# Queueing the weight-block sums of a decoder layer behind the attention's loads and products

## The chip, the cores and the metric

The kernel runs on one core of a Trainium2 chip. The metric is the device time of one launch in microseconds (us), lower is better. Times are medians of several runs. Profiles come from single executions, so each has its own time beside that median.

TensorE (PE) multiplies matrices and loads their weights (PEld), VectorE (DVE) and GpSimd (POOL) work elementwise, ScalarE (ACT) evaluates functions, and SyncE (SP) issues most of the DMA transfers. Each engine takes its instructions in the order of its own queue.

## The reference

One decoder layer in float32, with 2048 tokens of 1024 channels:

```python
a = rmsnorm(h, g_pre_mix);  u = a @ w_in
conv_out = swish(layernorm(causal_depthwise_conv(val * sigmoid(gate), width 31)))
attn_out = rmsnorm(stick_breaking(q, k, v))            # 8 heads of 64
h = h + rmsnorm(concat(conv_out, attn_out) @ w_out, g_post_mix)
f = rmsnorm(h, g_pre_ffn)
h = h + rmsnorm((silu(f @ w_gate) * (f @ w_up)) @ w_down, g_post_ffn)
```

Stick-breaking attention has no softmax. The weight of key s for query t is sigmoid(z_ts) times the product of 1 − sigmoid(z_tj) over the keys j between s and t. The feed-forward part has 2816 inner channels, so w_gate and w_up are 1024 × 2816 and w_down is 2816 × 1024.

## The kernel before

**Precision.** Float32 products are made from three matmuls: each operand is split into a rounded high part H and the rest L (ACT makes H, POOL or DVE makes L), and H·H + H·L + L·H is summed in PSUM.

**The feed-forward part** multiplies 2 × 2 blocks by a scheme of seven block products instead of eight. That takes sums and differences of blocks of the weights. For w_gate and w_up they are made early, by `sums` (line 839), while the attention runs. For each of 11 pairs j of column tiles and each of the two weights there is a group: `piece` (line 841) loads blocks of 128 × 512, 256 KB, into tiles with the tag `sum`, of which there are three (line 843 issues the load on SP's queue), `combine` (line 848) adds or subtracts two of them in place on POOL (line 849), and `flush` stores the result in DRAM (through `part`, line 777, on SP). A group is four loads, four combinations and four stores, so there are 88 of each. The blocks of the feed-forward part read the results back (line 1044).

**The attention.** `attn(g)` (line 536 and on) works through four groups g of 512 queries, eight heads each, and for each head through the key groups c from g down to 0. A pair of head and key group is called a unit; there are 8, 16, 24 and 32 units in the four groups, 80 in all. `fetch` (line 550) loads K and V of a unit on SP (lines 553 and 554), each with two buffers. `scores` (line 557) multiplies on PE (565, 566), takes two sigmoids on ACT (571, 573), a running product on DVE (575), and multiplies both on POOL (576), with small copies on POOL around it (570, 578). `values` (line 583) transposes the result on PE (592), splits it (249 on ACT, 250 on DVE) and multiplies it with V (597, 598).

**The convolution.** `taps` runs 31 multiply-adds per channel group on DVE (line 478), and `convnorm` (line 485) normalizes four token tiles, one after another: PE transposes (491), ACT and DVE, POOL (192, 193, 503), PE transposes back (508). All four go through one PSUM bank. The output projection of the convolution's half (691 to 693) needs the result of its group.

**What sets the order.** The program is traced in an order written by hand. PLAN lists the main stages with costs; the running sum of those costs is the position, from 0 to about 930. Three side streams, attention, taps and sums, are advanced beside the main stages, so that each has reached a given share of its own work at a given position: ATTN from 0 at position 46 to 1 at 850, SUMS from 0 at 330 to 1 at 900. Steps of the attention are traced before steps of the sums at each point.

From the traced order a scheduler lays out each engine's queue, using a simulated timeline. An instruction that can run and whose buffer is free may be put ahead of instructions that were traced before it. `tc.keep_in_program_order` holds some instructions to the traced order. The sums read only inputs, so in the queues nothing but their tiles holds them back.

The functions that the diff touches:

Of the kernel before, what the change touches and what calls it, by code (L numbers as in the profile page):

```python
# [9 lines left out]
F32 = mybir.dt.float32  # L10
# [3 lines left out]
ALU = mybir.AluOpType  # L14
# [14 lines left out]
G = 512  # L29
# [109 lines left out]
def layer_kernel(ctx: ExitStack, tc: tile.TileContext, x, xT, g_pre_mix, w_in, conv_w, conv_b, ln_g, ln_b,  # L139
                 attn_g, w_out, g_post_mix, g_pre_ffn, w_gate, w_up, w_down, g_post_ffn, out):  # L140
    nc = tc.nc
# [161 lines left out]
    for c in range(CB):  # L303
        t = vp.tile([P, PAD + G], F32, name=f"glu{c}")
# [5 lines left out]
    vd = {}  # L310
# [225 lines left out]
    def attn(g):  # L536
# [13 lines left out]
        def fetch(h, c):  # L550
            K = ap.tile([P, G], F32R, tag="K", name="K")
            V = ap.tile([P, G], F32R, tag="V", name="V")
            nc.sync.dma_start(K.bitcast(F32), kd[h, c].bitcast(F32))
            nc.sync.dma_start(V.bitcast(F32), vd[h // 2, c][:, h % 2, :].bitcast(F32))
            return dict(h=h, c=c, K=K, V=V, A=[])

        def scores(u, j):
            hd_ = heads[u["h"]]
            diag = u["c"] == g
            w = (j + 1) * P if diag else G  # L560
            K = u["K"]
            z = pp.tile([P, G], F32, tag="z", name="z")
            late = g == NG - 1 and u["h"] >= NH // 2
            js = slice(j * P, (j + 1) * P)
            nc.tensor.matmul(z[:, 0:w], hd_["QL"][:, js], K[:, 0:w], start=True, stop=False)
            nc.tensor.matmul(z[:, 0:w], hd_["QH"][:, js], K[:, 0:w], start=False, stop=True)
            if diag:
                nc.vector.tensor_tensor(z[:, w - P:w], z[:, w - P:w], msk, ALU.add)  # L568
            om = ap.tile([P, G + 9], F32, tag="om", name="om", bufs=NOM)
            nc.gpsimd.tensor_copy(om[:, G:G + 1], hd_["prev"][j])  # L570
            nc.scalar.activation(om[:, G - w:G], z[:, 0:w], AF.Sigmoid, scale=-0.125)  # L571
            a = ap.tile([P, G], F32, tag="A", name="A", bufs=NA)
            nc.scalar.activation(a[:, 0:w], z[:, 0:w], AF.Sigmoid, scale=0.125)  # L573
            r = om[:, G - w:G + 1][:, ::-1]
            nc.vector.tensor_tensor_scan(r, r, (one if late else z[:, 0:1]).to_broadcast([P, w + 1]), one, ALU.mult, ALU.bypass)  # L575
            nc.gpsimd.tensor_tensor(a[:, 0:w], a[:, 0:w], om[:, G - w + 1:G + 1], ALU.mult)  # L576
            pv = sp.tile([P, 1], F32, tag="pv", name="pv", bufs=8)
            nc.gpsimd.tensor_copy(pv, om[:, G - w:G - w + 1])
            hd_["prev"][j] = pv
            u["A"].append(a)  # L580
            return w
# [56 lines left out]
        for n in range(len(units) + 1):  # L638
            u = None
            if n < len(units):  # L640
                h, c = units[n]
                if c == g:
                    yield need(("q", g, h // 2), ("k", g, h // 2), ("v", g, h // 2))
                    heads[h] = begin(h)
                u = fetch(h, c)
            for i in range(TT):
                w = 0
                if u is not None:
                    w += scores(u, i)
                if last is not None:  # L650
                    w += values(last, i)
                later = [(k - 1, fn, a) for k, fn, a in later]
                while later and later[0][0] <= 0:
                    _, fn, a = later.pop(0)
                    if fn is back and g > 1:
                        yield need(("mix", g - 2))
                    fn(a)
                yield w
            if last is not None and last["c"] == 0:
                h = last["h"]  # L660
                oT = ap.tile([P, G], F32, tag="oT", name="oT", bufs=1)
                nc.scalar.activation(oT, heads[h]["o"], AF.Copy)
                heads[h]["oT"] = oT
                later.append((FOLD, fold_halves, h))
                if h % 2:
                    later.append((BACK, back, h))
            last = u
# [3 lines left out]
            fn(a)  # L671
        done.add(("attn", g))

    ys = {}

    def outproj(g, part):
# [92 lines left out]
    def store(t, *key, eng=nc.sync):  # L769
        stored[key] = dp.tile([P, *t.shape[1:]], F32, name="_".join(str(k) for k in key))  # L770
        eng.dma_start(stored[key], t)

    def part(t, k, n, *key, eng=nc.sync):

        if key not in stored:
            stored[key] = dp.tile([P, n, G], F32, name="_".join(str(k) for k in key))
        eng.dma_start(stored[key][:, k, :], t)
# [61 lines left out]
    def sums():  # L839

        def piece(w, j, e):
            t = fup.tile([P, G], F32, tag="sum", name="sum", bufs=3)
            nc.sync.dma_start(t, w[j][:, e * G:(e + 1) * G])
            return t

        late = []

        def combine(c, a, b, op, *key):
            nc.gpsimd.tensor_tensor(c, a, b, op)  # L849
            late.append((c, *key))  # L850

        def flush(n):
            while len(late) > n:
                t, kind, *key, m = late.pop(0)
                if kind == "S":
                    ns = (6, 7) if m in (6, 7) else (5, 3)
                    part(t, ns.index(m), 2, kind, *key, ns)
                else:
                    store(t, kind, *key, m)

        for j in range(HF):
            for i, w in enumerate(W):
                a21, a22, a11 = piece(w, j + HF, 0), piece(w, j + HF, 1), piece(w, j, 0)
                yield 1
                combine(a22, a21, a22, add, "S", i, j, 5)
                yield 1
                combine(a21, a21, a11, sub, "S", i, j, 7)
                combine(a11, a22, a11, sub, "S", i, j, 6)
                yield 1
                flush(0)  # L870
                a12 = piece(w, j, 1)
                yield 1
                combine(a12, a12, a11, sub, "S", i, j, 3)
                yield 1
                flush(0)
# [111 lines left out]
    with ExitStack() as E:  # L987
# [10 lines left out]
        e = [(ep, f"e{i}") for i in range(6)]  # L998
# [450 lines left out]
```

## Time and profile before

| | before |
|---|---|
| median of 3 runs | 2525.97 us (2524.9 to 2527.77) |
| the profiled execution, its own time | 2525.87 us |
| its span, first to last instruction | 2523.9 us |
| mean granted clock of PE | 0.981 |
| PE busy | 2392.2 us, 95% of the span |
| DVE, POOL, ACT busy | 1796.9, 1522.1, 1291.7 us |
| DMA | 657.31 MB, mean 260 GB/s |

The attention's units run from 64 to 1470 us of the span, beside the input projection (15 to 889), the output projection of each group and the first block products of the feed-forward part (c11, 915 to 1101 and 1284 to 1464, and p4, 1166 to 1256). After that come the remaining block products of w_gate and w_up (from 1517 to 2084) and those of w_down (2084 to 2514).

In a row of instructions, `L849` is the line of the kernel, `sum<-sum` the tile written and the tiles read, and `x88` the count. Idle time before a group is the time in which the engine had nothing running ahead of its instructions, with what ended it behind the arrow. PEclk, the granted clock, is the share of full speed at which TensorE was clocked in that stretch.

### The profile page before, as it was taken

To read this page: it belongs to the slowest core of one execution; us is meant where nothing else is said; L and a number is where in the kernel's file an instruction comes from. 1 tells how busy PE (TensorE), PEld (TensorE's weight loads), DVE (VectorE), ACT (ScalarE), POOL (GpSimd) and SP (SyncE) were. 2 spreads that over 40 slices of the span, in tenths; PEclk is the share of its full clock that TensorE was granted. 3 is DMA by queue.
4 is the path that set the end of the run, shared out by engine and by line. 5 is a ranking of instruction groups with operands and counts; after the bars stand their busy time and mean duration, and the time that the engine had idled before them with its cause. 6 is when DMAs were issued, how large, how long until landed. Compare 5 with 4: busy or idle time off the path is not lost. (4 is left out here: it accounts for less than half of the span.)

```text
span 2523.9 us, 35648 instructions
## 1 busy us (share of the span) xinstructions
PE 2392.2 (95%) x11156; PEld 1951.2 (77%) x11156; DVE 1796.9 (71%) x2321; ACT 1291.7 (51%) x2398; POOL 1522.1 (60%) x1845
## 2 busy tenths in 40 slices
PE   7989989998899999999989998999999999999998
PEld 6878777775687877888778877777788887887886
DVE  5797579886899887777877536776666654557556
ACT  4554565655565575676666745333332234445443
POOL 5764678547563376637745408765666674558656
PEclk9999999998899999999999999999999999999999
DMA  9989887987576689765677686987878767668765
GB/s 353 319 292 319 287 265 267 353 282 239 185 275 207 205 304 348 240 228 199 235 270 226 212 284 226 345 281 245 311 278 284 273 239 269 192 195 263 251 188 179
DMA packets 289181, 657.31 MB, mean 260 GB/s; under 512 B 33888, under 2 KB 42080, under 8 KB 288992
## 3 DMA queue, kind: packets, MB, share of 16 engines
q1 hardware_dynamic: 264704, 622.01, 73.2%
q10 hardware_dynamic: 24288, 33.04, 3.6%
q8 instruction: 88, 1.44, 0.2%
q14 instruction: 101, 0.83, 0.1%
HBM read 460.92 MB, written 193.99 MB: 259 GB/s over the span
## 5 line engine op out<-in xcount | busy, mean ns | idle before, releaser
L576 POOL TENSOR_TENSOR A<-A,om 128x512 f32<-128x512 f32 (+2 forms) x320 | 320.5, 1003 | 315.1 <-DVE om L575 233.9
L1056 POOL TENSOR_TENSOR wL<-raw,wH 128x512 fp32r<-128x512 f32 x176 | 254.7, 1469 | 193.8 <-ACT wH L1055 186.0
L478 DVE SCALAR_TENSOR_TENSOR cv<-glu,cw,cv 128x512 f32<-128x512 f32 x464 | 346.4, 747 | 5.7
L575 DVE TENSOR_TENSOR_SCAN om<-om,one,z 128x513 f32<-128x513 f32 (+3 forms) x256 | 277.5, 1097 | 70.9 <-ACT A L573 65.4
L1287 DVE TENSOR_TENSOR xL__22010<-t__22012,xH__22009 128x512 fp32r<-128x512 f32 x154 | 198.7, 1295 | 163.4 <-ACT xH__22009 L1286 163.4
L1285 POOL TENSOR_TENSOR xL__22008<-t__22011,xH__22007 128x512 fp32r<-128x512 f32 x154 | 211.3, 1379 | 158.9 <-ACT xH__22007 L1284 150.1
L257 PE MATMUL inps<-xH,wL 128*128 128x512 f32 x640 | 258.4, 404 | 6.1 <-ACT sg L424 5.5
L571 ACT ACTIVATE om<-z 128x512 f32<-128x512 f32 (+2 forms) x320 | 171.5, 537 | 177.4 <-DVE z L568 75.7
L261 PE MATMUL inps<-xL,wH 128*128 128x512 f32 x640 | 255.1, 400 | 0.0
L259 PE MATMUL inps<-xH,wH 128*128 128x512 f32 x640 | 254.8, 399 | 0.0
L250 DVE TENSOR_TENSOR TL<-at,TH 128x512 fp32r<-128x512 f32 (+1 forms) x320 | 188.8, 598 | 91.5 <-ACT TH L249 90.8
L765 PE MATMUL dps<-xH__22007,xL__22010 128*128 128x512 f32 x616 | 241.4, 392 | 5.1 <-DVE xL__22010 L1287 4.5
L765 PE MATMUL dps<-xL__22008,xH__22009 128*128 128x512 f32 x616 | 241.1, 391 | 1.4 <-POOL xL__22008 L1285 1.4
L765 PE MATMUL dps<-xH__22007,xH__22009 128*128 128x512 f32 x616 | 240.8, 391 | 0.0
L1284 ACT ACTIVATE xH__22007<-t__22011 128x512 fp32r<-128x512 f32 x154 | 97.2, 631 | 219.8 <-POOL xL__22008 L1285 117.2
L249 ACT ACTIVATE TH<-at 128x512 fp32r<-128x512 f32 (+1 forms) x320 | 167.7, 546 | 81.4 <-PE at L592 79.9
L592 PE MATMUL at<-idr,A 128*128 128x128 f32 x1088 | 188.9, 277 | 5.2 <-POOL A L576 3.6
L211 ACT ACTIVATE wH<-raw 128x1024 fp32r<-128x1024 f32 x156 | 165.9, 1064 | 39.5 <-DMA raw<-in_w_in_dram 20.8
L573 ACT ACTIVATE A<-z 128x512 f32<-128x512 f32 (+2 forms) x320 | 167.8, 539 | 32.9 <-PE at L592 32.9
L1055 ACT ACTIVATE wH<-raw 128x512 fp32r<-128x512 f32 x176 | 101.2, 623 | 162.3 <-PE b L765 52.8
L592 PEld LDWEIGHTS at<-idr,A 128*128 128x128 f32 x1088 | 140.3, 142 | 42.2 <-POOL A L576 5.4
L849 POOL TENSOR_TENSOR sum<-sum 128x512 f32<-128x512 f32 x88 | 114.8, 1305 | 84.8 <-DMA sum<-in_w_up_dram 32.9
(304 smaller groups left out, 6358.2 us busy)
## 6 DMA issues: line engine op xcount, KB each, us to landing
wL<-wL SPq DMA_DIRECT2D x156, 512.0 KB, 5.0
raw<-in_w_in_dram SPq DMA_DIRECT2D x80, 512.0 KB, 6.1
t__22012<-u SPq DMA_DIRECT2D x154, 256.0 KB, 2.8
c<-c ACTq DMA_DIRECT2D x88, 256.0 KB, 4.1
t__22011<-wd SPq DMA_DIRECT2D x88, 256.0 KB, 2.9
K<-kd SPq DMA_DIRECT2D x80, 256.0 KB, 4.7
V<-vd SPq DMA_DIRECT2D x80, 256.0 KB, 4.1
u<-accf SPq DMA_DIRECT2D x22, 768.0 KB, 4.5
```

What stands on the lines that cost most here:

```text
L250: nc.vector.tensor_tensor(L, ps, H.bitcast(F32), ALU.subtract)
L257: nc.tensor.matmul(ps, WL[:, kc], aH[t](k), start=k == 0, stop=False)
L259: nc.tensor.matmul(ps, WH[:, kc], aH[t](k), start=False, stop=False)
L261: nc.tensor.matmul(ps, WH[:, kc], aL[t](k), start=False, stop=k == KT - 1)
L478: nc.vector.scalar_tensor_tensor(to, gl[c][:, k:k + G], cw[:, c, k:k + 1], a, ALU.mult, ALU.add))
L575: nc.vector.tensor_tensor_scan(r, r, (one if late else z[:, 0:1]).to_broadcast([P, w + 1]), one, ALU.mult, ALU.bypass)
L576: nc.gpsimd.tensor_tensor(a[:, 0:w], a[:, 0:w], om[:, G - w + 1:G + 1], ALU.mult)
L592: nc.tensor.transpose(pt[:, j * P:(j + 1) * P], u["A"][j][:, b * P:(b + 1) * P], id32)
L765: return nc.tensor.matmul(ps, a, b, skip_group_check=True, **flags)
L1056: nc.gpsimd.tensor_tensor(l, t, f32(h), sub)
L1285: nc.gpsimd.tensor_tensor(WL, w, f32(WH), sub)
L1287: nc.vector.tensor_tensor(UL, t, f32(UH), sub)
```

## The change

Two instructions of the attention are remembered each time they are traced: the load of V and POOL's product. Each load of a block for the sums is traced inside `tc.issue_after(recent["sync"])`, each combination inside `tc.issue_after(recent["pool"])`. That context puts the instructions traced in it behind the given one in the queue of their common engine. It adds no semaphore and no wait at run time. The stores of the sums are not pinned; they follow the combinations through their data.

```diff
         def fetch(h, c):
...
-            nc.sync.dma_start(V.bitcast(F32), vd[h // 2, c][:, h % 2, :].bitcast(F32))
+            recent["sync"] = nc.sync.dma_start(V.bitcast(F32), vd[h // 2, c][:, h % 2, :].bitcast(F32)).ins
...
-            nc.gpsimd.tensor_tensor(a[:, 0:w], a[:, 0:w], om[:, G - w + 1:G + 1], ALU.mult)
+            recent["pool"] = nc.gpsimd.tensor_tensor(a[:, 0:w], a[:, 0:w], om[:, G - w + 1:G + 1], ALU.mult).ins
...
+    recent = {}
...
         def piece(w, j, e):
             t = fup.tile([P, G], F32, tag="sum", name="sum", bufs=3)
-            nc.sync.dma_start(t, w[j][:, e * G:(e + 1) * G])
+            with tc.issue_after(recent["sync"]):
+                nc.sync.dma_start(t, w[j][:, e * G:(e + 1) * G])
             return t
...
         def combine(c, a, b, op, *key):
-            nc.gpsimd.tensor_tensor(c, a, b, op)
+            with tc.issue_after(recent["pool"]):
+                nc.gpsimd.tensor_tensor(c, a, b, op)
             late.append((c, *key))
```

## The prediction

> **What bounds the kernel now.** I read the page first, then a table of stages, then the sums, then the waits. The page says that TensorE is the engine to watch and that little of it is free:
>
> ```profile
> span 2523.9 us, 35648 instructions
> PE 2392.2 (95%) x11156; PEld 1951.2 (77%) x11156; DVE 1796.9 (71%) x2321; ACT 1291.7 (51%) x2398; POOL 1522.1 (60%) x1845
> PE   7989989998899999999989998999999999999998
> PEclk9999999998899999999999999999999999999999
> ```
>
> PE stands idle for 2523.9 − 2392.2 = 131.7 us, and slices 10 and 11 (about 590 to 757 us) run at a lower granted clock as well. The stages show where that lies. Columns: stretch, length, busy us of PE, PEld, DVE, ACT, POOL (with counts), granted clock, share of the DMA engines, GB/s.
>
> ```profile
> 0.00:50.00 50.00, 40.55 (x171) 32.79 (x172) 28.05 (x39) 25.75 (x37) 30.05 (x47) 1.00 0.98 363
> 50.00:350.00 300.00, 278.74 (x1372) 227.80 (x1371) 219.72 (x358) 160.19 (x322) 187.97 (x280) 0.97 0.92 306
> 350.00:590.00 240.00, 226.49 (x1089) 184.04 (x1090) 207.84 (x307) 134.87 (x256) 156.17 (x239) 0.98 0.85 288
> 590.00:667.00 77.00, 52.61 (x214) 36.44 (x213) 58.32 (x80) 41.81 (x85) 54.12 (x85) 0.78 0.62 203
> 667.00:900.00 233.00, 224.12 (x1117) 182.69 (x1115) 210.59 (x301) 139.97 (x263) 113.71 (x211) 1.00 0.68 225
> 900.00:1000.00 100.00, 95.08 (x487) 77.36 (x488) 78.20 (x110) 62.62 (x118) 72.25 (x102) 0.98 0.96 338
> 1000.00:1236.00 236.00, 233.19 (x1147) 192.51 (x1145) 179.24 (x231) 155.33 (x291) 146.93 (x223) 1.00 0.68 226
> 1236.00:1300.00 64.00, 56.66 (x283) 45.56 (x284) 51.64 (x70) 41.31 (x78) 34.70 (x56) 0.95 0.80 277
> 1300.00:1430.00 130.00, 130.00 (x663) 108.13 (x663) 86.79 (x112) 87.33 (x162) 64.97 (x114) 1.00 0.69 224
> 1430.00:1517.00 87.00, 82.60 (x367) 66.12 (x366) 31.41 (x45) 46.58 (x74) 12.63 (x16) 0.96 0.78 263
> ```
>
> I call a stretch's loss its idle PE time plus (1 − clock) times its length. 50 to 590 loses 21.3 + 13.5 idle and 9.0 + 4.8 of clock: 48.6 us, 9.0% of 540. 590 to 667 loses 24.4 + 16.9 = 41.3 of 77. 667 to 1430 loses 8.9 + 4.9 + 2.8 + 7.3 + 0 idle and 2.0 + 3.2 of clock: 29.1 us, 3.8% of 763. So about 90 us lie where the sums run now, and 29 us where they will go.
>
> The sums' own answer (durations ns min/median/max, first and last start; then what POOL waited for ahead of a sum, us and times; then landing times of all transfers of the tile, loads and stores):
>
> ```profile
> L849 POOL TENSOR_TENSOR sum<-sum x88: 1261/1290/1741, 16.4 to 667.5; 128x512 f32<-128x512 f32 x88
> L843 SPq DMA_DIRECT2D sum<-in_w_gate_dram x44: 328/401/1138, 9.7 to 649.5; - x44
> L843 SPq DMA_DIRECT2D sum<-in_w_up_dram x44: 327/422/1079, 25.8 to 663.7; - x44
> ...
>   DMA sum<-in_w_up_dram: 32.9, 10
>   DMA sum<-in_w_gate_dram: 29.2, 12
>   issue: 16.4, 5
> ...
> DMA to landing us min/median/max: 2.0/4.8/8.8
> ```
>
> A sum costs POOL twice: 114.8 us of work in all (88 of about 1.3 us), and 62.1 us in which POOL, whose queue is in order, stood at a sum whose load had not landed (the group's whole idle time is 84.8 us by the page's row for L849, quoted next). The sums wait for nothing but their own loads, so the scheduler has put them as far forward as their three tiles allow: from 9.7 us, though the first is traced at position 330 of about 930.
>
> ```profile
> L849 POOL TENSOR_TENSOR sum<-sum 128x512 f32<-128x512 f32 x88 | 114.8, 1305 | 84.8 <-DMA sum<-in_w_up_dram 32.9 <-DMA sum<-in_w_gate_dram 29.2 <-issue 16.4
> ```
>
> **What the change moves, and where to.** Nothing is added or removed: 88 loads of 256 KB, 88 combinations, and through their data 88 stores of 256 KB. ATTN runs from position 46 to 850, SUMS from 330 to 900 in 22 groups of four loads and four combinations. At 330 the attention has done (330 − 46)/804 = 35.3% of its work. Its four groups weigh 10, 26, 42 and 58 of 136, so 48.0 of 136 is 12.0 of 42 into group 2: the second unit of head 2, which makes 8 + 16 + 6 + 2 = the 32nd of 80 loads of V. Position 850 is 20.07 groups, so the last two stand behind the 80th. In the trace the 32nd row of L554 and its last stand here:
>
> ```profile
> 628.69 0.32 SPq L554 DMA_DIRECT2D V<-vd  x1
> ```
>
> ```profile
> L554 SPq DMA_DIRECT2D V<-vd x80: 319/326/1077, 63.6 to 1428.6; - x80
> ```
>
> So all sums leave 10 to 629 us and spread over 629 to about 1460: one in 9.4 us instead of one in 7.5. V itself can't be pulled far forward, since it has two buffers that the attention must free. The context orders the queues and adds no wait at run time.
>
> **Gain, 590 to 667.** Here PE has only attention work, while the convolution's norm of group 1 (its four tiles go through one PSUM bank, with POOL steps at L192, L193 and L503) holds up the output projection. POOL's groups in this stretch:
>
> ```profile
> L576 POOL TENSOR_TENSOR A<-A,om 128x512 f32<-128x512 f32 (+3 forms) x20 | 21.3, 1066 | 6.4 <-DVE om L575 6.4
> L849 POOL TENSOR_TENSOR sum<-sum 128x512 f32<-128x512 f32 x15 | 20.0, 1333 | 18.2 <-DMA sum<-in_w_gate_dram 7.4 <-DMA sum<-in_w_up_dram 4.8 <-issue 3.3
> ```
>
> Sums take or hold 20.0 + 18.2 = 38.2 us of POOL's 77. Without them POOL has 34 us of work, and DVE with 58.3 is the next limit, so the stretch gives at most 77 − 58.3 = 18.7 us; at least 0, if DVE's order paces it anyway. The nearest row is the same norm in group 2, which runs beside no sum. First and last transposes of the two:
>
> ```profile
> L491 PE MATMUL lps<-idr,acc x16: 270/272/273, 567.7 to 624.6; 128*128 128x128 f32 x16
> ```
>
> ```profile
> L508 PE MATMUL cps<-idr,cs x16: 272/346/473, 582.2 to 642.2; 128*128 128x128 f32 x16
> ```
>
> ```profile
> L491 PE MATMUL lps<-idr,acc x16: 270/272/328, 858.7 to 912.6; 128*128 128x128 f32 x16
> ```
>
> ```profile
> L508 PE MATMUL cps<-idr,cs x16: 270/272/273, 873.7 to 925.8; 128*128 128x128 f32 x16
> ```
>
> 642.2 − 567.7 = 74.5 us beside sums, 925.8 − 858.7 = 67.1 without: I take 7.4 us. The lower clock of this stretch follows its gaps:
>
> ```profile
> 599.78 0.79 PE L598 MATMUL o<-TL,V 128*128 128x512 f32 x1 [5.54 <-DVE TL L250]
> 602.15 0.77 PE L565 MATMUL z<-K,QL 128*128 128x512 f32 x1
> ```
>
> After 5.54 us of waiting a matmul of 512 columns took 0.79 us, and 2 us later still 0.77. The Trainium skill (TensorE: Matmul & The Clock Gate, Part 1) says that the clock is halved after an idle window of about 3.4 us and comes back after as long a busy one. By that rule the 7.4 us stand only while such gaps remain; were they all to fall under the window, the clock's 16.9 us would come back too, and the sum below would be 16.9 us lower. The trace shows slow matmuls behind a 5.5 us gap, and no run here shows the threshold.
>
> **Gain, 50 to 590.** The sums' work and waits here are 114.8 − 20.0 and 84.8 − 18.2 us, less the few of the first 50 us, and the DMA engines are 85 to 92% busy, partly with 88 transfers out and back. If this stage came to the 3.8% that the later one loses, it would lose 20.5 us instead of 48.6: a gain of 28 at most. It is 0 if DVE (220 of 300 and 208 of 240 us) is what PE waits for in any case. I take 12, under half, because DVE is the second most loaded engine here and its taps and scans don't move.
>
> **Cost, 667 to 1430.** POOL gets 115 us of sums and whatever it waits for their loads, in front of the attention's products. Upper end: the stage loses 9.0% as the early one did, scaled by 7.5/9.4 for the thinner stream: 763 × (9.0% − 3.8%) × 0.8 = 32 us. Lower end 0: 1300 to 1430 has no idle PE at all with POOL at 65 of 130, as dense products of the feed-forward part always stand ready. I take 9, nearer to that row than to the early ones: 1000 to 1236, with POOL at 62%, idles 2.8 of 236. Loads of the sums come right behind V, not ahead of K or V. A load that waits for one of the three tiles does hold SP with K and the weights queued behind it; now SP stands at the stores behind POOL:
>
> ```profile
> SPq L777 <- POOL sum L849: 53.2, 35, 5.0
> ```
>
> That is 1.5 us each; K, V and the weights are loaded one or two steps ahead, which covers it. If that cover went, the 53 us would fall on PE in part, and that lies inside the upper end.
>
> **Cost, DMA in 900 to 1000.** The engines are 96% busy at 338 GB/s. Two and a half groups of 8 × 0.262 MB add 5.6 MB, 56 GB/s: 394, where the best row shows 363. The excess of 3.1 MB takes 8.6 us. It costs between 0 and 8.6; I take 2, because the stretch behind it runs at 68% and the loads are prefetched.
>
> **The end.** Two groups stand behind the last V load. POOL then has 12.6 us of work in 87, so they fit, and their results are read only by the last of eleven pairs of the blocks that begin at 1517. I price this at nothing; if those sums held up the loads of the output projection's weights on SP, one landing of 4.8 us would show at about 1464.
>
> **Sum.** −7.4 − 12 + 9 + 2 = −8.4 us. The profiled execution took 2525.87 us for its span of 2523.9, and the median is 2525.97, 0.1 us more, so no correction: 2517.5 us. A measurement here tells about 0.2%, 5 us, from no change.
>
> **Rivals.** First, slower: POOL in the attention of groups 2 and 3 waits at sums for loads, as it does now in the first 667 us. Three tiles for four loads mean that a group's fourth load starts only when a store has landed (4.8 us median), and the combination then stands at the head of POOL's queue in front of products that PE transposes. At the upper end: 32 + 2 − 19.4 = +14.6, 2540.5. It decides once the stage from 667 to 1430 loses over 19 us more than its 29. For it speaks that 62.1 us of such waits exist now; against it, the full PE from 1300 to 1430.
>
> Second, no change: DVE, not POOL, paces 50 to 590 (gain 5 instead of 12), or the DMA engines pay the 8.6 us in full. The first gives 2524.5, the second 2524.1. The Trainium skill (DMA: Bandwidth & Descriptors, Where 436 GB/s comes from) gives about 358 GB/s as one core's share of HBM bandwidth. By that limit the excess would be 36 GB/s and about 10 us, and my sum about 2525.5. The trace's 363 agrees within 2%, so the limit is real, but whether PE is behind it in 900 to 1000 is open.
>
> Third, more: the early stage falls to the later stage's loss and the later stage hides everything: −7.4 − 28 = −35, 2490.5. Against it: DVE's load. Fourth, the scheduler keeps the sums early after all: 2526; V's buffers make that improbable.
>
> **Chances.** Forecast 0.38 (2508 to 2520); slower 0.26; no change 0.20; more 0.14; not moved 0.02. So faster 0.52, same 0.22, slower 0.26. The forecast's own range is 2508 to 2520; to hold 8 in 10 the range goes into both outer rivals: 2494 to 2541.
>
> **What would show it.** Right: the sums run from about 629 to 1460; POOL's idle time ahead of sums is under 60 us; the norm of group 1 takes about 67 us; the loss up to 667 falls by about 20 us, and from there to 1430 grows by about 11. Wrong: POOL's waits at L849 stay at 62 us or more and move PE's waits to POOL's products after 667; or the loss up to 590 stays at 49; or c11's products from 900 on wait for weights.

## The result and the profile after

The changed kernel is slower: 2540.05 us median of 4 runs (2533.92 to 2543.27) against 2526.87 us (2524.9 to 2528.45) for the kernel before, a ratio of 1.0062 with a 95% interval of 1.0042 to 1.0081. The profiled execution, at 2533.92 us, is the fastest of the four, so its trace shows some 6 us less than the median does.

The page after, the same lines as before:

```profile
span 2532.1 us, 35646 instructions
PE 2391.7 (94%) x11156; PEld 1948.6 (77%) x11156; DVE 1801.4 (71%) x2321; ACT 1291.6 (51%) x2398; POOL 1529.7 (60%) x1845
PE   7989999998999899999899999999999999999998
PEclk9999999999999999999899999999999999999999
```

PE's busy time is the same to half a microsecond. The clock's dip at slices 10 and 11 is gone, and another low clock has come at slice 20 (1203 to 1266 us). The table of stages shows both sides of the exchange:

```profile
0.00:50.00 50.00, 37.09 (x153) 29.58 (x154) 24.81 (x35) 25.37 (x36) 25.75 (x42) 0.97 0.87 305
50.00:350.00 300.00, 278.38 (x1378) 229.64 (x1377) 215.57 (x356) 156.67 (x316) 141.06 (x244) 0.97 0.74 236
350.00:590.00 240.00, 224.97 (x1094) 181.26 (x1092) 213.18 (x317) 140.59 (x268) 123.60 (x221) 0.99 0.69 231
590.00:667.00 77.00, 68.82 (x321) 52.56 (x320) 65.82 (x97) 50.16 (x100) 39.76 (x73) 0.91 0.60 183
667.00:900.00 233.00, 219.92 (x1091) 178.18 (x1091) 203.27 (x287) 135.20 (x253) 132.89 (x219) 1.00 0.81 280
900.00:1000.00 100.00, 91.30 (x457) 73.46 (x458) 76.06 (x97) 58.30 (x110) 79.44 (x103) 0.98 0.92 327
1000.00:1236.00 236.00, 223.47 (x1080) 182.39 (x1080) 179.95 (x232) 151.57 (x285) 176.15 (x248) 0.99 0.78 266
1236.00:1300.00 64.00, 55.13 (x259) 43.51 (x258) 51.31 (x65) 37.90 (x71) 45.34 (x66) 0.89 0.84 295
1300.00:1430.00 130.00, 129.34 (x652) 106.98 (x651) 86.77 (x111) 83.84 (x154) 86.98 (x121) 1.00 0.87 296
1430.00:1517.00 87.00, 81.05 (x380) 65.34 (x379) 35.74 (x50) 52.39 (x87) 28.53 (x34) 0.98 0.91 314
```

From 590 to 667 PE ran 321 matmuls instead of 214. From 667 to 1430 it idled 43.8 us instead of 23.9 (add the differences of length and busy time). In the first 590 us POOL works 84 us less (374.2 before, 290.4 after) and the DMA engines' share, 0.85 to 0.98 by stretch before, is 0.69 to 0.87, yet PE gets no more done there.

To compare kernels at a time x, I add the columns of all matmuls that the trace shows started by x, divide by 2400, which gives a unit of about a microsecond of work, and subtract the same of the kernel before. I call the difference the lead. A matmul of 512 columns counts 0.213 us in this measure, and at full speed one starts every 0.227 us, so a unit of lead is worth about 1.07 us. The changed kernel's lead:

| at us | 50 | 350 | 590 | 667 | 850 | 1100 | 1300 | 1430 | 1517 |
|---|---|---|---|---|---|---|---|---|---|
| changed | −3.8 | −1.8 | −3.1 | 17.3 | 16.7 | 6.2 | −8.3 | −9.1 | −10.5 |

So the change wins 20 units in one stretch of 77 us, and loses 25 between 850 and 1300. The sums moved as the change says, except that the first group came sooner than I had worked out. The answer for the tile `sum` of the changed kernel:

```profile
L852 POOL TENSOR_TENSOR sum<-sum x88: 1267/1292/2337, 503.8 to 1470.8; 128x512 f32<-128x512 f32 x88
L845 SPq DMA_DIRECT2D sum<-in_w_gate_dram x44: 328/424/2138, 492.4 to 1446.5; - x44
L845 SPq DMA_DIRECT2D sum<-in_w_up_dram x44: 328/422/1369, 599.6 to 1465.9; - x44
```

SP's timeline of the changed kernel at the first group, right behind a load of V (start, us taken):

```profile
492.04 0.32 SPq L554 DMA_DIRECT2D V<-vd  x1
492.41 1.37 SPq L845 DMA_DIRECT2D sum<-in_w_gate_dram  x3
```

And POOL now hardly waits at a sum. By the group's row (busy us, mean ns, idle us ahead), the idle time fell from 84.8 to 16.3 us:

```profile
L852 POOL TENSOR_TENSOR sum<-sum 128x512 f32<-128x512 f32 x88 | 117.0, 1330 | 16.3 <-DMA sum<-in_w_up_dram 7.9 <-DMA sum<-in_w_gate_dram 7.9
```

### The profile page after: what moved, and what is told of

Same layout as the page of the kernel before. It is cut to its first block, busy times and chain, and to the rows that moved or that the text cites. A ratio compares the mean times of both kernels' runs of the same rounds, so it can differ in the third digit from the quotient of the medians.

```text
span 2532.1 us, 35646 instructions
## 1 busy us (share of the span) xinstructions
PE 2391.7 (94%) x11156; PEld 1948.6 (77%) x11156; DVE 1801.4 (71%) x2321; ACT 1291.6 (51%) x2398; POOL 1529.7 (60%) x1845
## 5 line engine op out<-in xcount | busy, mean ns | idle before, releaser
L565 PE MATMUL z<-K,QL 128*128 128x512 f32 (+2 forms) x320 | 129.3, 405 | 33.9 <-DVE om L575 21.2
```

## The experiments

Three theories. **Load**: what counts is where the sums' own work lies, on POOL or on the DMA engines and SP. **POOL against transfers** divides that theory in two. **Layout**: moving the sums makes the scheduler lay out all queues anew, and the time follows from that. The changed kernel and the twelve of the experiments, with their ratios to runs of the kernel before on the same chip (medians 2523.6 to 2526.9 us; a ratio is estimated from the runs and need not equal the quotient of two medians):

| run | median us | ratio, 95% interval | lead at 590 | 667 | 850 | 1100 | 1300 | 1517 |
|---|---|---|---|---|---|---|---|---|
| changed | 2540.05 | 1.0062 (1.0042 to 1.0081) | −3.1 | 17.3 | 16.7 | 6.2 | −8.3 | −10.5 |
| none | 2508.42 | 0.9945 (0.9921 to 0.9970) | −6.4 | 16.5 | 13.7 | 10.7 | 14.7 | 10.2 |
| no_combine | 2546.24 | 1.0090 (1.0066 to 1.0114) | 0.3 | 19.8 | 15.3 | −3.0 | −12.6 | −14.3 |
| combine_only | 2536.82 | 1.0050 (1.0035 to 1.0065) | −8.1 | 12.8 | 7.8 | 8.6 | 5.6 | −8.3 |
| quarter | 2526.40 | 0.9998 (0.9981 to 1.0016) | −4.1 | 17.0 | 7.4 | 6.8 | 8.3 | −2.1 |
| shift | 2543.80 | 1.0080 (1.0065 to 1.0095) | −2.9 | 19.2 | 13.7 | −0.4 | −5.4 | −18.3 |
| loads_only | 2550.59 | 1.0099 (1.0076 to 1.0123) | −1.5 | 16.6 | 9.0 | −4.6 | −7.8 | −22.2 |
| gap_pinned | 2561.53 | 1.0140 (1.0113 to 1.0166) | −8.7 | −3.4 | −10.3 | −24.3 | −18.1 | −28.4 |
| gap_free | 2532.93 | 1.0032 (1.0016 to 1.0047) | −1.2 | 6.5 | 5.4 | −12.9 | −11.0 | −7.7 |
| free_no_combine | 2511.35 | 0.9951 (0.9935 to 0.9968) | −2.4 | 18.1 | 12.6 | 12.2 | 14.4 | 10.5 |
| free_shift | 2523.00 | 0.9999 (0.9988 to 1.0010) | −2.1 | −0.2 | −0.3 | −1.5 | −1.1 | 0.0 |
| tail | 2519.76 | 0.9982 (0.9968 to 0.9996) | 0.2 | 8.3 | 7.1 | 8.1 | 9.8 | 4.5 |
| tail12 | 2561.64 | 1.0138 (1.0107 to 1.0169) | −3.4 | 2.7 | −4.9 | −11.0 | −11.6 | −19.4 |

### What the sums cost in all: none

```diff
         for j in range(HF):
             for i, w in enumerate(W):
+                if i or j:
+                    for ns in ((6, 7), (5, 3)):
+                        stored["S", i, j, ns] = stored["S", 0, 0, ns]
+                    for _ in range(5):
+                        yield 1
+                    continue
                 a21, a22, a11 = piece(w, j + HF, 0), piece(w, j + HF, 1), piece(w, j, 0)
```

> The changed kernel with only the first of the 22 groups of sums made; the blocks read that group's results for all pairs. The changed kernel lost what it had gained: its TensorE was about 17 us of work ahead of the kernel before at 667 us of the span and 8 us behind at 1300. Load theory (the sums, by POOL or by transfers, cost TensorE time beside the first block products, 850 to 1300 us): without them the lead of 17 us stays, so about 2507 to 2512 us. Layout theory (any move of the sums re-lays all queues, and the late loss is that, not the sums' own load): the loss between 667 and 1300 comes again, 2525 to 2545 us.

2508.42 us, and the lead of the changed kernel at 667 us stays to the end (16.5, then 14.7 at 1300). So with the sums gone from their early place and not done later the kernel is 16 us faster than before, and with them done later 13 us slower. This is what the load theory says. The run also prices the sums where the kernel before has them: the lead grows by 22.9 from 590 to 667, and nothing is won ahead of that, for the lead at 590 is −6.4.

### Which part costs it late: no_combine, combine_only, quarter

No combinations:

```diff
         def combine(c, a, b, op, *key):
-            with tc.issue_after(recent["pool"]):
-                nc.gpsimd.tensor_tensor(c, a, b, op)
             late.append((c, *key))
```

> The changed kernel without POOL's 88 combinations; all loads and stores remain, and the stores write the raw blocks. POOL theory (115 us of combinations stand in POOL's queue before the attention's products): the late loss goes, about 2512 to 2518 us. Transfer theory (loads and stores on SP and the DMA engines stand before the weights of the first block products): the late loss stays, 2532 to 2542 us.

Combinations alone, where `only` is the pinned combination without a store, and the group's five yields stay:

```diff
+                if i or j:
+                    for ns in ((6, 7), (5, 3)):
+                        stored["S", i, j, ns] = stored["S", 0, 0, ns]
...
+                    only(a22, a12, a22, add)
...
+                    only(a12, a12, a11, sub)
+                    only(a11, a22, a11, sub)
...
+                    only(a12, a12, a11, sub)
...
+                    continue
```

> The changed kernel with the 88 combinations at their places on POOL, but loads and stores of the first group alone; later combinations run on that group's tiles, and the blocks read that group's results. POOL theory: the late loss stays, 2532 to 2542 us. Transfer theory: it goes, 2510 to 2518 us.

2546 and 2537 us: each part alone gives nearly the whole slowdown, so neither theory as I had set them against each other stands. The places differ. Here are 850 to 1100 us, the first block products of the feed-forward part, with columns as in the table of stages, for none, no_combine and combine_only in this order:

```profile
850.00:1100.00 250.00, 240.09 (x1204) 197.91 (x1203) 184.26 (x248) 160.73 (x298) 157.47 (x225) 0.97 0.81 278
```

```profile
850.00:1100.00 250.00, 229.52 (x1133) 185.94 (x1132) 181.82 (x241) 150.19 (x281) 156.44 (x228) 0.96 0.89 307
```

```profile
850.00:1100.00 250.00, 240.70 (x1212) 196.27 (x1211) 180.93 (x246) 160.28 (x296) 180.26 (x242) 1.00 0.83 282
```

With transfers and no combinations PE ran 71 matmuls fewer than with neither. With combinations and no transfers it ran 8 more, though POOL worked 180 us instead of 157. So in this stretch the transfers cost PE's time and POOL does not. What combine_only loses, it loses at the end. The stretch 1430 to 1517 of combine_only, where the row of before in the prediction has 82.60 us of PE's work, 366 weight loads and 12.63 us of POOL's:

```profile
1430.00:1517.00 87.00, 74.10 (x324) 57.87 (x323) 45.42 (x53) 50.96 (x85) 41.11 (x44) 0.92 0.64 218
```

Of POOL's 41 us, 14.0 are nine sums and some 20 the attention's steps. The attention's last matmul of line 598 ends at 1482.4 us, and in none, without these combinations, at 1450.9. The last block product ends at 1450.6, so for 32 us PE has only the attention and the output projection. In the kernel before the two ends are 6.4 us apart (1470.3 and 1463.9).

The transfers with a quarter of their bytes, and no combinations:

```diff
-                nc.sync.dma_start(t, w[j][:, e * G:(e + 1) * G])
+                if first[0]:
+                    nc.sync.dma_start(t, w[j][:, e * G:(e + 1) * G])
+                else:
+                    nc.sync.dma_start(t[:, 0:P], w[j][:, e * G:e * G + P])
...
+                if not first[0]:
+                    nc.sync.dma_start(dump[m % 4], t[:, 0:P])
+                    continue
```

> As the run without combinations (2546 us), but from the second group on each load and store moves 128 of 512 columns, 64 KB instead of 256 KB, with as many instructions on SP at the same places; the blocks read the first group's results. Bandwidth theory (the transfers' 46 MB crowd the weights of the first block products on DMA engines that are 80 to 96% busy there): about 2510 to 2520 us, near the 2508 of the run with one group. Queue theory (the loads and stores hold SP, with the weights, K and V behind them): 2535 to 2550 us.

2526 us lies between the two forecasts, halfway from none to no_combine. From 850 to 1300 the loss is gone: the lead goes from 7.4 to 8.3, where no_combine fell from 15.3 to −12.6. Both issue 43 stores of the sums there, and 43 (no_combine) and 45 (quarter) loads. So there it is bytes and not instructions on SP, and this holds for 1100 to 1300 as well. The two rows, first no_combine, then quarter, with 149 matmuls between them:

```profile
850.00:1300.00 450.00, 413.33 (x2015) 332.60 (x2013) 338.48 (x440) 279.79 (x530) 281.65 (x419) 0.97 0.83 289
```

```profile
850.00:1300.00 450.00, 432.69 (x2164) 352.93 (x2163) 343.88 (x457) 292.15 (x550) 280.95 (x425) 0.99 0.79 270
```

All runs side by side say the same of 850 to 1100. The six kernels with the sums' full transfers in that stretch (changed, no_combine, shift, loads_only, gap_pinned, gap_free) lose 10.5 to 18.3 there, with the DMA engines at 0.87 to 0.91. The other seven go from −6.1 to +1.0, at 0.80 to 0.85.

What is left of quarter's loss comes at 667 to 850 and at 1430 to 1517. In the second, 8.8 us are one wait of PE, at the output projection's first product (line 692) for DVE's split of its operand (line 529), when the block products have ended (1452.4 us); the same wait takes 4.4 us in none and 8.7 in loads_only. What made it longer I can't assign, nor the loss at 667 to 850, where free_no_combine and gap_pinned lose 5.5 and 6.9 without a sum in the stretch.

### How much is layout: shift, loads_only, free_shift

```diff
-SUMS = ((330, 0.0), (900, 1.0))
+SUMS = ((345, 0.0), (900, 1.0))
```

This one line was applied to the changed kernel (shift) and to the kernel before (free_shift). In loads_only the changed kernel's `combine` is the old one, without the context.

> The changed kernel with the sums' line begun at position 345 instead of 330, which moves each group by a few microseconds at most. Load theory: 2537 to 2543 us, as the changed kernel. Layout theory: it can land anywhere within about 10 us of the changed kernel, and the difference says how much of any single comparison is layout.

> The kernel before with the sums' line begun at position 345 instead of 330. Nothing holds the sums to their traced place, so their load stays where it was: 2524 to 2529 us if a time follows the load alone. The distance from the kernel before is what re-laying the queues does by itself; over 5 us would say that single comparisons of that size prove nothing.

> One part of the change alone: the loads are pinned behind V, the combinations are free. Since a combination needs its load, nothing moves far: 2535 to 2545 us, as the changed kernel, by either theory. If the place of each combination behind a product were the cost, about 2520 to 2528 us.

Where the sums are free, the shift moved nothing: 0.9999, and the lead is never beyond 2.1 in the table. But this is no test of the layout theory: by line and tile, the instructions of PE, DVE, ACT and POOL and SP's transfers start in the same order in this trace as in that of the kernel before, so no queue was laid out anew. The run shows how far two traces of one order differ, about 2 units. In the pinned kernel the shift did change the queues. It left the sign and size (1.0080, within the changed kernel's interval) but moved the place: less loss at 1100 to 1300, and 13 units at 1430 to 1517. loads_only is slower, as the changed kernel is, so the place of a combination behind a product is not the cost. Its median is 10 us higher than the changed kernel's, and the intervals just overlap.

### Which stretches cost: free_no_combine, gap_pinned, gap_free, tail, tail12

The kernel before without combinations, the same edit to line 849:

> The kernel before (nothing pinned) without POOL's 88 combinations: loads and stores run early as before, and the stores write the raw blocks. If the norm of group 1 and the output projection behind it were late because sums held POOL (38 of 77 us between 590 and 667), the stretch gives its 20 us of TensorE work back without them: 2506 to 2514 us. If the transfers of the first 600 us held it up, about 2520 to 2528 us.

2511 us, with the whole gain at 590 to 667 (−2.4 to 18.1) although all transfers run early. This points to POOL. It isn't a clean split, since without combinations the loads ran ahead and the last one starts at 509 us, before the norm. But in the kernel before the DMA engines stand at only 0.62 in this stretch, and its trace shows the norm's short steps on POOL held up by sums. For the second of the four tiles, the step of line 193 starts 4.5 us after the end of the one before it (line 192), since a sum lies between them, ahead of which POOL stood idle for 3.27 us. In the changed kernel the same two steps start 0.8 us apart (585.15 and 585.98 us).

```profile
592.12 0.19 POOL L192 TENSOR_SCALAR msc<-mv 128x1 f32<-128x1 f32 x1
595.58 1.26 POOL L849 TENSOR_TENSOR sum<-sum 128x512 f32<-128x512 f32 x1 [3.27 <-issue]
596.80 0.55 POOL L193 TENSOR_TENSOR mv<-msc,nhalf 128x1 f32<-128x1 f32 x1
```

The norm of group 1, first and last transpose, takes 622.1 − 571.6 = 50.5 us here, and 621.2 − 560.9 = 60.3 us in the changed kernel, against 74.5 before. The groups' rows (durations in ns, then first and last start in us), two of free_no_combine and then two of the changed kernel:

```profile
L491 PE MATMUL lps<-idr,acc x16: 270/272/273, 571.6 to 612.6; 128*128 128x128 f32 x16
```

```profile
L508 PE MATMUL cps<-idr,cs x16: 270/272/328, 582.3 to 622.1; 128*128 128x128 f32 x16
```

```profile
L491 PE MATMUL lps<-idr,acc x16: 270/272/273, 560.9 to 612.5; 128*128 128x128 f32 x16
```

```profile
L508 PE MATMUL cps<-idr,cs x16: 270/272/421, 575.2 to 621.2; 128*128 128x128 f32 x16
```

What the lead at 667 us follows in all runs is the time at which this norm ends: 618.5 to 626.5 us in the eight kernels with a lead of 12.8 to 19.8, 633.2 and 635.1 in tail and gap_free (8.3 and 6.5), 642.2 in the kernel before, 652.5 in gap_pinned (−3.4). It is shorter wherever few sums or none run beside it (50.5 to 63.4 us), but its start moves too, between 557 and 588 us, and that is not only a matter of sums near it.

Then kernels with the sums in other places. gap_pinned changes only the line; the others leave the first groups free and pin the rest:

```diff
-SUMS = ((330, 0.0), (900, 1.0))
+SUMS = ((116, 0.0), (282, 0.65), (442, 0.65), (552, 1.0))                    # gap_pinned
+SUMS = ((330, 0.0), (442, 0.63), (552, 1.0))                                 # gap_free
+SUMS = ((330, 0.0), (442, 0.63), (723, 0.63), (783, 0.75), (910, 1.0))       # tail
+SUMS = ((330, 0.0), (414, 0.45), (723, 0.45), (783, 0.63), (910, 1.0))       # tail12
...
-            with tc.issue_after(recent["sync"]):
+            with tc.issue_after(recent["sync"]) if "late" in recent else ExitStack():
...
+                if 2 * j + i == 14:                                           # 10 in tail12
+                    recent["late"] = True
```

> All sums, pinned as in the changed kernel, but with a line that puts 14 groups at positions 116 to 282 (about 150 to 500 us), none from 282 to 442 and 8 at 442 to 552 (about 670 to 890 us). Load theory (what counts is where the sums' POOL work and transfers lie: they cost beside the norm of group 1 at 560 to 667 us and beside the first block products from 850 on, and nothing to speak of elsewhere): 2505 to 2515 us. Layout theory: 2525 to 2545 us.

> The first 14 groups not pinned, so that the scheduler puts them forward as in the kernel before, and the last 8 pinned at positions 442 to 552. Load theory: 2505 to 2515 us. If pinning as such costs something, this is faster than the run with all pinned by more than 5 us. Layout theory: 2525 to 2545 us.

Both missed. The groups that I meant for 670 to 890 us ran later, since the attention's loads of V that they follow are themselves later than I took them to be: the first pinned load stands behind the 43rd load of V, at 827 us in gap_free. In gap_free (POOL's busy time of the sums alone):

```profile
667.00:850.00 183.00, 5.11 (x4) 0.99 0.70 241
850.00:1100.00 250.00, 30.62 (x24) 0.97 0.87 303
```

They met the very stretch that no_combine had named, and the lead fell there by 18, from 5.4 to −12.9. In gap_pinned 17 sums ran between 500 and 600 us and 22 between 850 and 1050: it won only 5.3 at 590 to 667, and lost 14.0 from 850 to 1100. The next run moves the same eight groups out of that stretch:

> 14 groups free as in the kernel before, 8 pinned from position 723 on, so that they run from about 1240 us to the end of the attention, not beside the first block products of 850 to 1100 us. The run with the same 14 free groups and 8 at 800 to 1150 us took 2533 us and lost about 17 us of TensorE work in that stretch. Load theory: those 17 us come back, less up to 8 for the attention at 1236 to 1300 us: 2515 to 2525 us, and no loss between 850 and 1100 us. Layout theory: 2525 to 2545 us, with losses anywhere.

The sums' POOL time in tail, by the same view:

```profile
590.00:850.00 260.00, 0.00 (x0) 0.95 0.59 196
850.00:1100.00 250.00, 0.00 (x0) 0.99 0.83 281
1100.00:1300.00 200.00, 5.14 (x4) 0.98 0.70 235
1300.00:1517.00 217.00, 37.12 (x28) 0.98 0.86 299
```

2519.76 us, as the load theory had it, with no loss from 850 to 1100 (7.1 to 8.1): the same groups cost 18 there and at most 5 at the end, from 1300 to 1517, where none loses 4.5 without them. tail is the fastest kernel here that makes all sums, faster than the kernel before by 0.04 to 0.32%.

> As the run with 8 groups pinned at the end of the attention (2520 us), with 10 groups free and 12 pinned from position 723 on. Load theory: the free groups are done by about 340 us instead of 450, so the norm of group 1 comes earlier and the lead at 667 us grows from 8 to 10 to 17 us of TensorE work; the twelve cost the attention at 1236 to 1300 us and at its end up to 10 us. So 2512 to 2522 us; more than 2526 us would say that the end has no room for twelve.

2561.64 us: the end has no room for twelve. Sums still ran after 1550 us, and the lead fell from −16.4 at 1430 to −35.2 at 1700. But this run also counts against the load theory. No sum runs between about 345 and 1290 us, and yet it lost 13.7 between 667 and 1100 us (2.7 to −11.0). At 590 to 667 it won 6.1 where gap_free won 7.7 with four groups more in front: its norm of group 1 takes only 60.3 us, but starts at 584.0 and ends at 644.3. From 590 to 850 us PE's wait at an attention score for DVE's scan grew. PE's waits there (us in total, times, longest), of tail and then of tail12:

```profile
PE z L565 <- DVE om L575: 8.9, 15, 1.9
```

```profile
PE z L565 <- DVE om L575: 13.8, 24, 2.2
```

Neither has a sum there, so this is layout or comes down from what the layout did earlier, and why it came out so I can't say. It sets the measure: a loss of 14 can come without any sums beside it. The loss of 25 to 28 from 850 to 1300 us in the changed kernel and no_combine is beyond that, a loss of 5 to 10 in one stretch is not.

## Why the prediction was wrong

**Where the sums go.** Right for the end (1470.8 us against about 1460), off for the start. I took the line's 330 as the first group's position. The lines are read only at the ends of PLAN's stages, and the stage 282 to 392 goes in a straight line to its end value, so the first group was traced at 282, behind the 24th V and not the 32nd: 492 us instead of 629. That cost the sum little, since the second group followed only at about 600. A smaller slip is that slices 10 and 11 of the page are 568 to 694 us, not 590 to 757; the stretch that I priced lies inside them.

**Gain, 590 to 667.** Right in mechanism, too small: 7.4 us forecast, 20 measured, above the bound of 18.7 that I had put there. POOL's sums in front of the norm's steps are the cause as far as free_no_combine and the trace can show it. The norm took 60.3 us, not 67, and its first transpose came 6.8 us sooner, which I had not priced. The bound failed because it took DVE's 58.3 us as a fixed amount of work for the stretch. DVE worked 65.8 us of the 77 after, as the stretch simply had room for more of everything.

**Gain, 50 to 590.** Wrong: 12 us forecast, none measured (lead −3.8 at 50 us and −3.1 at 590). The loss by the prediction's own measure is 48 us after and 48.6 before, which was one of its signs of being wrong. POOL lost 84 us of work, the DMA engines had a fifth less to do, and PE got no further in any run without early sums (−6.4 in none). My lower bound, that PE waits for something else here, was the right one; what it waits for no run tests.

**Cost, 667 to 1430.** This is the step that failed: 9 + 2 us forecast, 26 measured. I had priced it from the stretches 1300 to 1430 and 1000 to 1236, where PE hardly idles, and in the first of them the sums do cost almost nothing (lead −8.3 to −9.1). The cost lay in the stretches that I had averaged away. From 850 to 1100 it is the transfers: 10.5 in the changed kernel, 18 in no_combine and in gap_free, none in tail, quarter and combine_only. I had seen that the stage stands at 96% of DMA and taken 2 of 8.6 us. That the weights are loaded ahead did not hide it, though the engines' mean share there after the change is only 0.91. From 1100 to 1300 the changed kernel lost another 14.5. That bytes have a part in it is shown by quarter, which lost nothing there where no_combine lost 9.7; how large it is stays open, for shift lost 5.0 in the same stretch and more at the end. In the changed kernel PE waits there at an attention score for ACT and at p4's products for the part L of their weights, which POOL makes, where the kernel before has 0.5 us and nothing:

```profile
PE z L565 <- ACT A L573: 6.0, 3, 5.0
PE p L766 <- POOL wL L228: 4.8, 4, 1.9
```

ACT, whose queue holds the attention's sigmoids too, also stood longer at p4's weights: 6.6 + 1.3 = 7.9 us before, 13.1 + 7.4 = 20.5 us after. The answers for line 227, ACT's conversion of these weights, have what it waited for (us and times), first of the kernel before, then of the changed one:

```profile
  DMA raw<-in_w_up_dram: 6.6, 3
  DMA raw<-in_w_gate_dram: 1.3, 3
```

```profile
  DMA raw<-in_w_gate_dram: 13.1, 5
  DMA raw<-in_w_up_dram: 7.4, 5
```

These waits don't decide it, though: quarter has 17.1 us of them and gap_pinned 21.4, and neither lost in this stretch.

**The rivals.** The first rival gave 2540.5 us and 2540.05 was measured, but not by its mechanism. POOL's waits at sums fell from 62.1 us on loads to 15.8, while the time went up. A right number beside a wrong cause is chance. In no stretch of the table after, from 667 to 1517, did the kernel move more than 327 GB/s on average, and the loss came at that rate. The limit of about 358 GB/s that the second rival weighed (the Trainium skill, DMA: Bandwidth & Descriptors, Where 436 GB/s comes from) was thus not reached there. Nor is the 363 GB/s of the first 50 us a sign that it is real, as I wrote: ten of them, of the kernel before, stand at 414:

```profile
30.00:40.00 10.00, 10.00 (x46) 8.29 (x45) 9.61 (x14) 4.47 (x8) 8.14 (x9) 1.00 1.03 414
```

With fewer gaps from 590 to 667 the stage's mean granted clock rose from 0.78 to 0.91, which is 10 of its 77 us and part of why the gain there was above my bound. The clock rule that the prediction weighed (the Trainium skill, TensorE: Matmul & The Clock Gate, Part 1) agrees with that, though no run shows its threshold.

**What stays open.** How the transfers, with the DMA engines at 87 to 91% from 850 to 1100, turn into PE's idle time, wait by wait, since PE's own rows name DVE's scans there. And how much of a pinned kernel's time is layout: between shift, loads_only and the changed kernel it is some 4 to 10 us, and tail12 lost 13.7 where no sums ran. No run changes the layout and keeps the load where it was.

## What to carry to other kernels

Before moving background work from one stage to another, price it in each stretch that it will enter, not by the mean or by the calmest: here the same eight groups cost 18 us beside the first block products and 5 us or less at the end. An engine's idle share in the stage that is left says little about the gain: 540 us with 9% of PE's time lost gave nothing back, while a 77 us stretch in which POOL's short steps formed a serial chain gave 20. Where a scheduler re-lays the queues, a control has to be seen to have re-laid them: free_shift looked like proof that layout costs nothing, and its queues were those of the kernel before.

## What was not expected of the hardware

Halving a cost into its two resources did not halve it: loads and stores alone cost 38 us against none, combinations alone 28, both together 32 (differences of the medians). Each seems to delay a different stream, transfers the dense products and POOL the attention, and when both streams are late by the same amount, PE can still fill one with the other. The ends of the two streams fit that reading (attention 1482.4 and block products 1450.6 us in combine_only, 1475.4 and 1474.5 in the changed kernel), but no run tests it.
